# Loading the first x tile as two column halves from two queues, both ahead of the opening barrier

## The chip, the cores and the metric

One core of a Trainium2 chip. The metric is the device time of one execution in microseconds (us). The program runs on a single core.

## The reference

```python
def setup_inputs():
    batch, seq, dim = 32, 256, 1024
    return {"x": randn(batch, seq, dim) as float32, "y": the same shape}

def reference(x, y):
    result = zeros((batch, seq, dim * 2), float32)
    result[..., 0::2] = x
    result[..., 1::2] = y
    return result
```

67 MB are read and 67 MB written. There is no arithmetic, only an interleave.

## The kernel before

The flat arrays are cut into eight blocks of 128 rows of 8192 numbers (32 KB a row, 4 MB a tile). SyncE issues the loads and ScalarE the stores; VectorE writes x and y into the even and odd places of an output tile, twice for each block. The x, y and output pools have two buffers each. At the program's start stands an opening barrier, at which the engines wait for one another; the first x load is issued ahead of it.

```python
    WL = 8192
    WS = 4096
    ...
    zero = wpool.tile([16, 128], fp32, name="zero")
    nc.vector.memset(zero, 0.0)
    first = dataclasses.replace(of, offset=0, ap=[[2 * WL, 16], [1, 128]])
    nc.scalar.dma_start(out=first, in_=zero)      # small early store, overwritten later

    start = 0
    for lw in lwidths:                            # 8 x 8192
        xtile = xpool.tile([P, WL], fp32, name="xtile")[:, :lw]
        ytile = ypool.tile([P, WL], fp32, name="ytile")[:, :lw]
        xs = dataclasses.replace(xf, offset=start, ap=[[lw, P], [1, lw]])
        ys = dataclasses.replace(yf, offset=start, ap=[[lw, P], [1, lw]])
        nc.sync.dma_start(out=xtile, in_=xs)
        nc.sync.dma_start(out=ytile, in_=ys)
        soff = 0
        while soff < lw:                          # two output tiles a block
            ...
            nc.vector.tensor_copy(out=otile[:, 0::2], in_=xsub)
            nc.vector.tensor_copy(out=otile[:, 1::2], in_=ysub)
            nc.scalar.dma_start(out=os_, in_=otile)
            soff += width
        start += P * lw
    ...
    # after scheduling: the first SyncE load is moved ahead of SyncE's
    # arrival at the opening barrier
    opening.insert(gate, moved)
```

Of the kernel before, what the change touches and what calls it, by code (L numbers as in the profile page):

```python
# [3 lines left out]

# [4 lines left out]


@with_exitstack
def _interleave(
    ctx: ExitStack,
    tc: tile.TileContext,
    x: bass.AP,
    y: bass.AP,
    out: bass.AP,
):
    nc = tc.nc  # L20
    P = 128

    total = 1
    for s in x.shape:
        total *= s

    WL = 8192
    WS = 4096

    xf = x.rearrange("b s d -> (b s d)")  # L30
    yf = y.rearrange("b s d -> (b s d)")
    of = out.rearrange("b s d -> (b s d)")

    fp32 = mybir.dt.float32

    xpool = ctx.enter_context(tc.tile_pool(name="xp", bufs=2))
    ypool = ctx.enter_context(tc.tile_pool(name="yp", bufs=2))
    opool = ctx.enter_context(tc.tile_pool(name="op", bufs=2))

    lwidths = [WL] * (total // P // WL)  # L40
    assert sum(lwidths) == total // P


    wpool = ctx.enter_context(tc.tile_pool(name="wp", bufs=1))
    zero = wpool.tile([16, 128], fp32, name="zero")
    nc.vector.memset(zero, 0.0)  # L46
    first = dataclasses.replace(of, offset=0, ap=[[2 * WL, 16], [1, 128]])
    nc.scalar.dma_start(out=first, in_=zero)

    start = 0  # L50
    for lw in lwidths:
        xtile = xpool.tile([P, WL], fp32, name="xtile")[:, :lw]
        ytile = ypool.tile([P, WL], fp32, name="ytile")[:, :lw]

        xs = dataclasses.replace(xf, offset=start, ap=[[lw, P], [1, lw]])
        ys = dataclasses.replace(yf, offset=start, ap=[[lw, P], [1, lw]])
        nc.sync.dma_start(out=xtile, in_=xs)
        nc.sync.dma_start(out=ytile, in_=ys)

        soff = 0  # L60
        while soff < lw:
            width = min(WS, lw - soff)
            otile = opool.tile([P, 2 * WS], fp32, name="otile")[:, : 2 * width]
            os_ = dataclasses.replace(
                of,
                offset=2 * start + 2 * soff,
                ap=[[2 * lw, P], [1, 2 * width]],
            )
            xsub = xtile[:, soff : soff + width]
            ysub = ytile[:, soff : soff + width]  # L70
# [6 lines that stand above are left out]
    assert start == total  # L77


def kernel(tc, x, y, out):  # L80
    nc = tc.nc
    _interleave(tc, x, y, out)
    tc.close()
    tc.compile()  # L84


    blocks = nc.main_func.blocks
    opening = blocks[0].instructions
    at, moved = next(
        (b, i)  # L90
        for b in blocks[1:]
        for i in b.instructions
        if i.engine == mybir.EngineType.SP and i.opcode == "DMACopy"
    )
    assert not moved.sync_info.on_wait
    body = at.instructions
    body.remove(moved)
    gate = next(
        n
        for n, i in enumerate(opening)  # L100
        if i.engine == mybir.EngineType.SP and i.opcode == "Drain"
    )
    opening.insert(gate, moved)
    at.instructions = body
    blocks[0].instructions = opening




    last = nc.main_func.blocks[-1]  # L110
    tail = last.instructions
    wait = tail[0]
    clear = next(n for n, i in enumerate(tail) if i.opcode == "ISA")
    assert wait.engine == mybir.EngineType.SP and wait.opcode == "Drain"
    assert wait.sync_info.on_wait and not wait.sync_info.on_update
    assert tail[clear].engine == mybir.EngineType.Pool
    last.instructions = [
        copy.replace(wait, engine=mybir.EngineType.Pool)
    ] + tail[clear:]


# [1 line left out]
_INS = ['x', 'y']  # L123
_OUTS = [((32, 256, 2048), 'float32')]


# [23 lines left out]
```

## Time and profile before

| | before |
|---|---|
| time, median of the first 3 runs | 316.17 us (315.44 to 316.24) |
| span in the profile | 313.6 us |
| 16 DMA engines, both queues | 99.6% of the span |
| mean rate, and from 30 to 310 us | 428 and 434 GB/s |
| VectorE | 23% |

The first line is the whole execution, the second the profiled one from the first to the last instruction. The third line is the one that counts: the packets that the DMA engines move fill next to all of the span, so a change gains only if it takes idle time or work from them. The lines behind this table are in the prediction.

### The profile page before, as it was taken

What the parts mean: (1) busy time and instruction counts of PE and PEld (TensorE: products, weight loads), DVE (VectorE), ACT (ScalarE), POOL (GpSimd) and SP (SyncE); (2) the same over time, 40 slices, a digit from 0 to 9 for tenths busy, and PEclk for the clock granted to TensorE, in tenths of its full rate; (3) what the DMA queues carried; (4) which work ended last, traced back from release to release, by engine and by line L of the source; (5) the groups of instructions that cost most, each with busy time, mean ns of one, the idle gap of its engine ahead of it and who ended that gap; (6) DMA issues with size and microseconds to landing.
All of it is one profiled execution on the core that took longest, in us unless ns stands there. A gap on an engine that the chain in (4) does not pass through costs nothing.

```text
span 313.6 us, 140 instructions
## 1 busy us (share of the span) xinstructions
DVE 72.8 (23%) x33; POOL 0.2 (0%) x4
## 2 busy tenths in 40 slices
DVE  0433002231022410325003150131501305023500
POOL 0000000000000000000000000000000000000000
DMA  8999999999999999999999999999999999999997
GB/s 344 460 405 397 464 405 464 405 464 405 460 410 447 422 439 431 435 435 426 443 410 460 401 468 401 468 401 464 405 464 405 464 405 460 410 447 422 439 431 334
DMA packets 4640, 134.23 MB, mean 428 GB/s; under 512 B 528, under 2 KB 544, under 8 KB 544
## 3 DMA queue, kind: packets, MB, share of 16 engines
q1 hardware_dynamic: 2304, 67.11, 50.0%
q10 hardware_dynamic: 2336, 67.12, 49.6%
HBM read 67.11 MB, written 67.12 MB: 428 GB/s over the span
## 4 chain that ended last, share of the span: by engine, by line
DMA 83%; DVE 11%; DVEq 1%; issue 0%
DMA out_dram<-otile 76%; DMA ytile<-in_y_dram 7%; DVE otile L72 6%; DVE otile L71 5%; DVEq L84 1%; DVEq L71 0%
## 5 line engine op out<-in xcount | busy, mean ns | idle before, releaser
L71 DVE COPY otile<-xtile 128x4096 f32<-128x4096 f32 x16 | 36.6, 2295 | 184.8 <-DMA out_dram<-otile 173.6
L72 DVE COPY otile<-ytile 128x4096 f32<-128x4096 f32 x16 | 36.6, 2292 | 39.8 <-DMA ytile<-in_y_dram 39.8
L46 DVE MEMSET zero<- 16x128 f32 x1 | 0.2, 165 | 0.9 <-PEq L134 0.9
L134 POOL MEMSET const-bfloat16-1.0<- 128x1 bf16 x1 | 0.1, 101 | 0.0
L134 POOL MEMSET const-uint8-127<- 128x1 uint8 x1 | 0.1, 101 | 0.0
L134 POOL MEMSET const-float32-0.0<- 128x1 f32 x1 | 0.1, 98 | 0.2 <-issue 0.2
L134 POOL MEMSET const-float32-1.0<- 128x1 f32 x1 | 0.1, 98 | 0.0
## 6 DMA issues: line engine op xcount, KB each, us to landing
out_dram<-otile ACTq DMA_DIRECT2D x16, 4096.0 KB, 29.1
xtile<-in_x_dram SPq DMA_DIRECT2D x8, 4096.0 KB, 43.6
ytile<-in_y_dram SPq DMA_DIRECT2D x8, 4096.0 KB, 60.7
out_dram<-zero ACTq DMA_DIRECT2D x1, 8.0 KB, 6.3
```

Source lines behind the costliest of these rows:

```text
L46: nc.vector.memset(zero, 0.0)
L71: nc.vector.tensor_copy(out=otile[:, 0::2], in_=xsub)
L72: nc.vector.tensor_copy(out=otile[:, 1::2], in_=ysub)
L84: tc.compile()
L134: nc = _bacc.Bacc("TRN2", target_bir_lowering=False, num_devices=1)
```

## The change

The intent is a quicker start. The first x tile is the first thing that the kernel needs, and one queue brings it. With two queues, each with a half and each issued before the barrier, the data might flow sooner. The small zero store moves behind ScalarE's half.

```diff
-    nc.scalar.dma_start(out=first, in_=zero)
 ...
-        nc.sync.dma_start(out=xtile, in_=xs)
+        if start == 0:
+            for q, c in ((nc.sync, 0), (nc.scalar, lw // 2)):
+                q.dma_start(
+                    out=xtile[:, c : c + lw // 2],
+                    in_=dataclasses.replace(xf, offset=c, ap=[[lw, P], [1, lw // 2]]),
+                )
+            nc.scalar.dma_start(out=first, in_=zero)
+        else:
+            nc.sync.dma_start(out=xtile, in_=xs)
         nc.sync.dma_start(out=ytile, in_=ys)
 ...
-    (move the first load of SP ahead of the barrier)
+    for engine in (mybir.EngineType.SP, mybir.EngineType.Activation):
+        (move that engine's first load ahead of the barrier)
```

More of the change, by code (lines that the diff above doesn't have):

```diff
@@ L87 @@
     blocks = nc.main_func.blocks
-    opening = blocks[0].instructions
-    at, moved = next(
-        (b, i)
-        for b in blocks[1:]
-        for i in b.instructions
-        if i.engine == mybir.EngineType.SP and i.opcode == "DMACopy"
-    )
-    assert not moved.sync_info.on_wait
-    body = at.instructions
-    body.remove(moved)
-    gate = next(
-        n
-        for n, i in enumerate(opening)
-        if i.engine == mybir.EngineType.SP and i.opcode == "Drain"
-    )
-    opening.insert(gate, moved)
-    at.instructions = body
-    blocks[0].instructions = opening
+    for engine in (mybir.EngineType.SP, mybir.EngineType.Activation):
+        opening = blocks[0].instructions
+        at, moved = next(
+            (b, i)
+            for b in blocks[1:]
+            for i in b.instructions
+            if i.engine == engine and i.opcode == "DMACopy"
+        )
+        assert not moved.sync_info.on_wait
+        body = at.instructions
+        body.remove(moved)
+        gate = next(
+            n
+            for n, i in enumerate(opening)
+            if i.engine == engine and i.opcode == "Drain"
+        )
+        opening.insert(gate, moved)
+        at.instructions = body
+        blocks[0].instructions = opening
     last = nc.main_func.blocks[-1]
```

## The prediction

> **What bounds the kernel now.** The kernel moves 67 MB in, interleaves, and moves 67 MB out. I read the page first: busy time of the engines, the 40 slices, the queues.
>
> ```profile
> span 313.6 us, 140 instructions
> DVE 72.8 (23%) x33; POOL 0.2 (0%) x4
> DMA  8999999999999999999999999999999999999997
> q1 hardware_dynamic: 2304, 67.11, 50.0%
> q10 hardware_dynamic: 2336, 67.12, 49.6%
> HBM read 67.11 MB, written 67.12 MB: 428 GB/s over the span
> ```
>
> VectorE, the only computing engine, is busy for 23% of the span. The two DMA queues (q1 is SyncE's with the loads, q10 ScalarE's with the stores) together take 50.0 + 49.6 = 99.6% of the time of all 16 DMA engines. Only the first and the last slice are under nine tenths. So before any chain is looked at, the transfers are the bound, and the question is how much of the span they don't use. I next asked for stretches of the span (columns: stretch, VectorE, GpSimd, clock, DMA share, GB/s).
>
> ```profile
> 0.00:3.50 3.50, 0.17 (x1) 0.20 (x4) 1.00 0.88 300
> 3.50:24.00 20.50, 6.55 (x3) 0.00 (x0) 1.00 1.01 435
> 24.00:30.00 6.00, 2.44 (x2) 0.00 (x0) 1.00 0.92 350
> 30.00:310.00 280.00, 63.62 (x28) 0.00 (x0) 1.00 1.00 434
> 310.00:313.60 3.60, 0.00 (x0) 0.00 (x0) 1.00 0.49 209
> ```
>
> From 30 to 310 us the 16 engines are full at 434 GB/s with no gap. Below that rate are the start, a short stretch around 27 us, and the last microseconds. For these I read the trace's packet records one by one. A packet carries 32 KB, and past 30 us all 3,728 of them take 1.213 us. Each engine has 4096 / 16 = 256 of them, 256 x 1.213 = 310.5 us. The rest of the span: the first packet starts 0.99 us after the first issue; the first packets take about 1.9 us, 0.7 too long; around 27 us one packet per engine takes about 1.8 us, 0.6 too long (there the first large store joins the loads); from the last data packet's end at 312.70 to the end at 313.57 are 0.9 us. 310.5 + 1.0 + 0.7 + 0.6 + 0.9 = 313.7, against 313.6: the span is accounted for. Only 1.0 + 0.7 = 1.7 us of it are start-up.
>
> Then the start in order of time (start, length, engine, what).
>
> ```profile
> 0.00 0.37 SPq L57 DMA_DIRECT2D xtile<-in_x_dram  x1
> ...
> 0.78 0.33 SPq L58 DMA_DIRECT2D ytile<-in_y_dram  x1
> ...
> 1.06 0.42 ACTq L48 DMA_DIRECT2D out_dram<-zero  x1
> 1.16 0.42 SPq L57 DMA_DIRECT2D xtile<-in_x_dram  x1
> 1.63 0.51 SPq L58 DMA_DIRECT2D ytile<-in_y_dram  x1
> 12.23 4.50 DVE L71 COPY otile<-xtile 128x4096 f32<-128x4096 f32 x2 [11.20 <-DMA xtile<-in_x_dram]
> ...
> 21.95 4.50 DVE L72 COPY otile<-ytile 128x4096 f32<-128x4096 f32 x2 [5.22 <-DMA ytile<-in_y_dram]
> 24.27 33.70 ACTq L73 DMA_DIRECT2D out_dram<-otile  x3
> ```
>
> The first x load is already issued at 0.00, ahead of the barrier; y follows at 0.78. The x tile's copies run from 12.23 to 16.7 us, then VectorE waits 5.22 us for y, and only the y copies let the first store go. The chain of waits says the same: it goes through the first y load, not through x.
>
> ```profile
> 0.78 21.14 DMA ytile<-in_y_dram
> 21.92 0.02 issue
> 21.95 4.51 DVE otile L72 x2
> 26.45 0.02 issue
> 26.47 40.91 DMA out_dram<-otile
> ```
>
> **What the Trainium skill says.** "DMA: Bandwidth & Descriptors", section "Issuing engines are not separate DMA queues": transfers issued by the scalar and sync engines run on the same 16 DMA engines and interleave; issuing from several saves only the time of the sequencer's issue. The trace agrees: both queues' packets appear on the same engines, and an issue takes 0.33 to 0.51 us. The same page, section "Queues, rings and completion order": each DMA engine takes turns between queues by packets. The trace agrees in part: around 30 us packets of q1 and q10 alternate one by one, but a newly filled queue comes in late, the zero store issued at 1.06 shows its first packets at 5.27, and the first large store issued at 24.27 at 29.07. The same page, section "Where 436 GB/s comes from", has a ceiling of 435.2 GB/s; the 434 GB/s measured over 280 us is 99.7% of it, so the middle has nothing to give.
>
> **The change part by part.**
>
> Start of the data. The first x load (4 MB, 128 rows of 32 KB) becomes two of 2 MB, each with 128 rows of 16 KB. SyncE's half is issued at 0.00 as the whole was. Each half still has 128 rows, so I expect an issue of some 0.37 us for each, perhaps 0.42 where both are at it, as the overlapping zero store (ScalarE) and second x load (SyncE) show with 0.42 each. ScalarE stands at the barrier at 0.13 us in the raw instruction records, so its half goes out at 0.0 to 0.15. The first packet can't come sooner than SyncE's did, 0.99 us after its issue. The long first packet is a latency, and a second queue beside it helps only if its data come within the same latency. The packets of one queue already follow each other without a gap (first ends and second starts agree to some ns), so the engine had the next packet ready already. I credit 0.2 us out of the 1.7, with 0 to 0.5 possible.
>
> More packets. The records give 27 ns for a 512-byte packet and 1.213 us for 32 KB: 1186 ns for 32256 bytes more, so 27.2 bytes per ns and 8.2 ns fixed (an estimate from these two). Each engine gets 16 x-packets of 16 KB in place of 8 of 32 KB: 8 x 8.2 = 66 ns more, and one more completion packet of 9 ns: +0.08 us.
>
> Barrier. ScalarE arrives there some 0.4 us later than now. But SyncE itself arrives late now for the same reason: its issue ends at 0.37 and its drain at 0.55. So the release, now at about 0.7, moves by 0.05 to 0.2 us, and with it y's issue. The x halves keep the DMA engines busy for 4.19 MB / 434 GB/s = 9.7 us. Hidden entirely: 0.
>
> Landing of x. Both halves share the engines, so x as a whole lands near 12.2 us as now. If ScalarE's queue comes in late, as the records show for a new queue, its half lands up to 2 or 3 us later and y packets go first. Then the second x copy would end at about 17 to 18 us; the slack before y is 5.2 us. Cost 0, and no gain either if x is early. y needs the same 8.4 MB ahead of its end and lands at about 21.9 as now.
>
> Zero store. It moves behind ScalarE's x half, and lands perhaps at 13 to 16 us in place of 7.4. ScalarE's first large store waits for it, but goes only at 24.27: 8 us of slack, cost 0. The copies, the 16 stores and the other 15 loads keep their order and waits; the instruction order of the built kernel shows nothing else moved.
>
> Sum: -0.2 + 0.08 = -0.1 us.
>
> **The rivals.** (1) The intent comes true: two queues fill the engines sooner, all of the 0.7 us of first-packet excess goes, or the 0.6 at 27 us goes since ScalarE's queue has then carried large packets before. For it: the 27 us pause comes exactly where that queue first carries much. Against it: the zero store has used the queue already, and what is new at 27 us is a large read from SBUF and write to HBM, which the change leaves. Time if both went: 316.17 - 1.3 = 314.9. (2) A lost start: ScalarE reaches its issue late, or the two issues hold each other up (0.42 against 0.33), the barrier slips and the halves interleave badly. Every known term lies under the 9.7 us of queued x, so at most some 0.5 us: 316.7. (3) A new order of packets makes the DMA engines run dry later, or the first store late: the slack of 5.2 us ahead of y speaks against it, and SyncE's queue already holds the second x and y, 8.4 MB or 19 us of work. If y came 2 us later after all, the loads behind would still fill the engines; 316 to 317.
>
> **Range and chances.** The three runs of before are 315.44, 316.24 and 316.17, mean 315.95, so the median stands at the upper end of its own scatter of 0.8 us. From 315.95 the -0.1 leads to 315.9 (315.85 rounded). The range takes the scatter of about 0.5 on either side and 0.3 for the start: 315.1 to 316.7. Two per cent are 6.3 us, while all that isn't streaming at full rate is 3.1 us: faster by over 2% is not to be had by anything that leaves the bytes as they are. Slower by 2% would need the DMA engines idle for 6 us. One chance in a hundred for each.
>
> **What would show it.** In the profile after: issues of both halves in the first 0.6 us, y's issue at 0.8 to 1.0; x complete at 12 to 15 us; VectorE still waiting for y, with y complete at 21.5 to 22.2; the first store issued within 0.5 us of 24.3; 434 GB/s from 30 to 310 us; a span of 313.0 to 314.0. The pause at 27 us should still be there. Wrong would be: a DMA share under 0.95 anywhere between 4 and 24 us, an x half that lands after y, a span shorter by over 1 us (then the first packets or the 27 us pause were the cost of a fresh queue), or a drop in the steady rate.

## The result, and the profile after

The changed kernel takes 315.70 us in the median of 6 runs (315.48 to 315.91), the kernel before 316.21 in the same rounds (315.44 to 316.38). The ratio is 0.9989, with a 95% interval of 0.9977 to 1.0002. Ratios here are the mean time of one kernel's runs over that of the other's of the same rounds, so not quite the ratio of the medians. The interval holds 1, and a second set of rounds (below) gave 1.0001. The time is the same.

The page after, the same lines as were read before:

```profile
span 313.8 us, 141 instructions
DMA  8999999999999999999999999999999999999997
q10 hardware_dynamic: 2480, 69.22, 51.1%
q1 hardware_dynamic: 2304, 65.01, 48.4%
```

2.1 MB moved from q1 to q10, that is, ScalarE's half. The sum is 99.5% where it was 99.6%. The span is 0.2 us longer in this one profiled execution, not shorter. By stretches (stretch, VectorE, GpSimd, clock, DMA share, GB/s):

```profile
0.00:3.50 3.50, 0.17 (x1) 0.20 (x4) 1.00 0.74 239
3.50:24.00 20.50, 6.44 (x3) 0.00 (x0) 1.00 1.03 442
24.00:30.00 6.00, 2.56 (x2) 0.00 (x0) 1.00 0.96 360
30.00:310.00 280.00, 63.60 (x28) 0.00 (x0) 1.00 1.00 433
310.00:313.80 3.80, 0.00 (x0) 0.00 (x0) 1.00 0.58 250
```

The long middle is unchanged, 433 against 434 GB/s. The first stretch looks worse (0.74 against 0.88) and the second better (1.03 against 1.01). Both come from how the view counts: a packet (one record of the trace, a row of 32 KB or here also of 16 KB that one DMA engine moves) is put down to the moment it starts, and with 16 KB packets fewer bytes have "started" by 3.5 us. Counted by the time that the packets really ran, the share up to 3.5 us is 0.64 before and 0.65 after. For such short stretches the packet records are the better witness, and they show a first packet at 1.02 us (0.99 before) and 0.64 us too much for each engine in the first packets (0.65 before). Such an excess is the time of all packets over the usual 1.213 or 0.611 us, summed and divided by 16, as the records carry no engine's number. The start in order of time:

```profile
0.00 0.37 SPq L59 DMA_DIRECT2D xtile<-in_x_dram  x1
0.12 0.38 ACTq L59 DMA_DIRECT2D xtile<-in_x_dram  x1
...
0.92 0.33 SPq L66 DMA_DIRECT2D ytile<-in_y_dram  x1
...
11.72 4.50 DVE L79 COPY otile<-xtile 128x4096 f32<-128x4096 f32 x2 [10.55 <-DMA xtile<-in_x_dram]
...
22.06 4.49 DVE L80 COPY otile<-ytile 128x4096 f32<-128x4096 f32 x2 [5.85 <-DMA ytile<-in_y_dram]
24.39 33.74 ACTq L81 DMA_DIRECT2D out_dram<-otile  x3
```

The second queue did go out early, at 0.12 us. VectorE could start on x 0.5 us earlier (11.72 against 12.23), and then waited 5.85 us for y in place of 5.22. But that was the first half alone. The two halves landed so (page, section 6: KB, us from issue to landing):

```profile
xtile<-in_x_dram SPq DMA_DIRECT2D x1, 2048.0 KB, 11.7
xtile<-in_x_dram ACTq DMA_DIRECT2D x1, 2048.0 KB, 13.4
```

ScalarE's half was thus there at 0.12 + 13.4 = 13.5 us, and x as a whole 1.3 us later than before (12.2). y is complete at 22.06 in place of 21.95, and the first store leaves 0.12 us later. The chain of waits still goes through the first y load, whose issue the barrier now holds 0.14 us longer:

```profile
0.92 21.12 DMA ytile<-in_y_dram
22.04 0.02 issue
```

So the first half of x came 0.5 us sooner and the second 1.3 us later, and neither mattered: no output tile can be stored before y is there, and y came at 22.0 us, when 8.4 MB had gone through the 16 engines.

### The profile page after: what moved, and what is told of

Its sections match the earlier page's. It is cut to its first block, busy times and chain, and to the rows that moved or that the text cites. A ratio compares the mean times of both kernels' runs of the same rounds, so it can differ in the third digit from the quotient of the medians.

```text
span 313.8 us, 141 instructions
## 1 busy us (share of the span) xinstructions
DVE 72.8 (23%) x33; POOL 0.2 (0%) x4
## 4 chain that ended last, share of the span: by engine, by line
DMA 83%; DVE 11%; DVEq 1%; issue 0%
DMA out_dram<-otile 76%; DMA ytile<-in_y_dram 7%; DVE otile L80 6%; DVE otile L79 5%; DVEq L92 1%; DVEq L79 0%
## 6 DMA issues: line engine op xcount, KB each, us to landing
xtile<-in_x_dram SPq DMA_DIRECT2D x1, 2048.0 KB, 11.7
xtile<-in_x_dram ACTq DMA_DIRECT2D x1, 2048.0 KB, 13.4
out_dram<-zero ACTq DMA_DIRECT2D x1, 8.0 KB, 14.8
```

## The experiments

The theory: the end is set by the bytes and packets that the 16 DMA engines have to move, plus 3 us in which they don't. Which queue brings the bytes, and when x, y or the first store come, is of no account as long as the engines never run dry. The main rivals: the second queue does gain something at the start; the chain through the first y load is the bound; splitting costs something.

**The split without the second queue.** Both halves from SyncE, both ahead of the barrier.

```diff
-            for q, c in ((nc.sync, 0), (nc.scalar, lw // 2)):
+            for q, c in ((nc.sync, 0), (nc.sync, lw // 2)):
...
-    for engine in (mybir.EngineType.SP, mybir.EngineType.Activation):
+    for engine in (mybir.EngineType.SP, mybir.EngineType.SP):
```

> The split alone: both halves of the first x tile from SyncE's queue, both ahead of the barrier; ScalarE issues nothing early. Theory (the DMA engines are full from the first packet on, and which queue carries the bytes is of no account): same time as before and as the change within 0.3 us; ratio to before 0.998 to 1.001; the halves complete one after the other, near 7.3 and 12.2 us, and y near 22.0. Rival (the second queue is what gained the 0.1%): as slow as before, 316.2, and the change's 315.7 not reached. Rival (the split costs): 316.5 or more.

Measured: 315.51 us (5 runs), ratio 0.9993 (0.9981 to 1.0005). The halves were in use at 7.53 and 12.26 us, y at 21.97. From one queue both halves thus land sooner than from two (11.7 and 13.5 us). The theory's numbers hold, and the rival that credits the second queue falls: with one queue the time is no longer.

**No early issue at all.** The kernel before without its move ahead of the barrier; the block that moves the load is deleted.

```diff
-    opening = blocks[0].instructions
-    at, moved = next(...)
-    ...
-    blocks[0].instructions = opening
```

> The kernel before with the early issue taken out: the first x load goes out after the barrier like everything else. Control for what a start of the data is worth. Theory: the start of the data moves by 0.6 to 0.8 us and nothing absorbs it, so the time grows by 0.6 to 0.8 us (ratio 1.002 to 1.0025). Rival (a start is absorbed by the slack in front of y or in the buffers): same time within 0.2 us.

Measured: 316.23 us, before 315.72 on the same chip; ratio 1.0013 (1.0001 to 1.0025), that is 0.0 to 0.8 us longer, 0.4 in the middle. x is issued at 0.73 us, the first packet starts at 1.72 in place of 0.99, and the last data packet ends at 313.55 in place of 312.70. In the traces the shift passes through whole: from the first packet to the end of the last are 311.8 us here and 311.7 before, so nothing made the late start good. In the times somewhat less of it shows, with an interval that holds the expected 0.6 to 0.8 but also the rival's 0.2 and less. So the rival of a start that is absorbed loses by the two traces; by the times alone it isn't excluded. The change didn't move the start of the data: SyncE's load was at 0.00 already.

**y ten microseconds later.** The changed kernel with the second x load ahead of the first y load.

```diff
             nc.scalar.dma_start(out=first, in_=zero)
+            ahead = xpool.tile([P, WL], fp32, name="xtile")[:, :lw]
+            nc.sync.dma_start(out=ahead, in_=(second x block))
         nc.sync.dma_start(out=ytile, in_=ys)
```

> The changed kernel with the second x load issued ahead of the first y load, so that y completes 9.7 us later (near 31.7 us) and the first store leaves near 34 instead of 24.4. Theory (only the filling of the DMA engines counts): the loads in the queue still cover the time until the stores come, the time stays within 0.5 us of the change, ratio to before 0.997 to 1.003. Rival (the chain of waits through the first y load is the bound, as the page prints it): 9.7 us longer, near 325.5, ratio 1.03.

Measured: 315.49 us (6 runs), ratio 0.9992 (0.9980 to 1.0004). Its start in order of time:

```profile
11.97 4.50 DVE L87 COPY otile<-xtile 128x4096 f32<-128x4096 f32 x2 [10.80 <-DMA xtile<-in_x_dram]
...
32.02 4.50 DVE L88 COPY otile<-ytile 128x4096 f32<-128x4096 f32 x2 [15.56 <-DMA ytile<-in_y_dram]
34.35 0.36 ACTq L89 DMA_DIRECT2D out_dram<-otile  x1
```

y comes 10.0 us later, the first store leaves 10.0 us later, and the time doesn't change. So the chain as the page prints it isn't the bound. It says what each instruction waited for, but the DMA engines were at other loads all that time. This is the plainest of the runs: if 10 us at this spot cost nothing, neither the 0.1 us that y lost nor the 0.5 us that the first half of x won can matter.

**Without the zero store.**

```diff
-            nc.scalar.dma_start(out=first, in_=zero)
```

> The changed kernel without the small zero store. Theory: the x half has already used ScalarE's queue and the zero store now lies off every path, so same time within 0.3 us, and the pause near 27 us (0.6 to 0.8 us of long packets for each engine) stays. Rival (the zero store is a first write that warms the way to memory): the pause near 27 us grows and the time with it, by 0.5 us or more.

Measured: 315.46 us, ratio 0.9991 (0.9979 to 1.0003); long packets near 27 us of 0.82 us for each engine, 0.78 in the change. The zero store warms nothing that can be seen here, and its move behind the x half costs nothing.

**The change once more.**

> The changed kernel once more, beside the runs of before on this chip, to narrow the ratio. Theory (nothing moved that the end depends on): ratio 0.998 to 1.001, median 315.4 to 316.0. Rival (a real gain of 0.5 us from the early second queue): ratio at or under 0.9985.

Measured: 315.88 us (315.65 to 316.01), before 315.56 in the same rounds; ratio 1.0001 (0.9986 to 1.0016). The rival of a real gain of 0.5 us falls, if only just: the interval reaches from 0.4 us faster to 0.5 slower. A gain as small as the 0.2 us that the prediction credits could not be seen in these times. The 316.21 of before in the first rounds was one of its own: the medians of before in four sets are 316.21, 315.72, 315.56 and 315.71.

**All loads in halves.** A large dose of the one cost that the prediction gave the change.

```diff
-        else:
-            nc.sync.dma_start(out=xtile, in_=xs)
-        nc.sync.dma_start(out=ytile, in_=ys)
+        for tile_, flat in ((xtile, xf), (ytile, yf)):
+            (not the first x tile, which is in halves already)
+            for c in (0, lw // 2):
+                nc.sync.dma_start(out=tile_[:, c : c + lw // 2], in_=(that half))
```

> The changed kernel with all the other 15 loads cut in two column halves as well, both from SyncE's queue: a large dose of the one cost that the prediction gave the change. Theory (a packet costs 8.2 ns beside its bytes, a completion 9 ns): each DMA engine gets 15 x 8 = 120 more packets and 15 more completions, 0.98 + 0.14 = 1.1 us, so near 316.8 and ratio to before 1.0035 (1.002 to 1.005); the 16 KB packets take 0.611 us. Rival (packets of 16 KB are free, the fixed part overlaps): same time within 0.3 us. Rival (shorter packets are much worse): over 2 us.

Measured: 322.41 us (4 runs), ratio 1.0207 (1.0187 to 1.0226), 6.5 us more. The 16 KB packets do take 0.611 us, as expected, but that makes 1.1 us. The expectation was wrong: something else came in. Two things had changed beside the packets. With 15 more transfers SyncE's loads share completion semaphores with stores (a semaphore is a counter that a transfer raises when it has landed, and for which an instruction can wait). The load issued at 39.56 us, for one, waits for semaphore 105, which the store issued at 19.68 raises. SyncE's waits show it (what waits, for what: us in all, times, longest):

```profile
SPq L68 <- DMA out_dram<-otile: 122.0, 12, 16.9
```

And a load packet is now half as long as a store packet. The last two runs below were made to tell these apart.

**A wider zero store.** 8 KB in each of its rows in place of 512 bytes.

```diff
-    zero = wpool.tile([16, 128], fp32, name="zero")
+    zero = wpool.tile([16, 2048], fp32, name="zero")
-    first = dataclasses.replace(of, offset=0, ap=[[2 * WL, 16], [1, 128]])
+    first = dataclasses.replace(of, offset=0, ap=[[2 * WL, 16], [1, 2048]])
```

> The changed kernel with the zero store widened from 512 bytes to 8 KB in each of its 16 rows (0.13 MB more to write, 0.3 us at 434 GB/s). Asks what the pause at the first large store is. Theory a (a cost of the first store packets of some size, which an early store can pay while x loads run): the pause of 0.65 to 0.8 us for each engine shrinks below 0.3 us there. Theory b (it belongs to the first large store whatever went before): the pause stays at 0.6 to 0.85 us. Either way the time stays within 0.5 us of the change, since the early store then pays it instead.

Measured: 315.93 us, ratio 1.0007 (0.9991 to 1.0022); the pause near 27 us is 0.72 us for each engine. It can't be paid ahead in this way. Theory b fits here, though not all that follows: see below.

**The intent taken further.** The whole x from SyncE and the whole y from ScalarE, both ahead of the barrier.

```diff
+        nc.sync.dma_start(out=xtile, in_=xs)
+        if start == 0:
+            nc.scalar.dma_start(out=ytile, in_=ys)
+            nc.scalar.dma_start(out=first, in_=zero)
+        else:
+            nc.sync.dma_start(out=ytile, in_=ys)
```

> The intent taken further: the whole first x load from SyncE and the whole first y load from ScalarE, both ahead of the barrier, 8.4 MB in two queues in place of 4.2. Theory (only the filling of the DMA engines counts): x and y share the engines and complete together near 20 to 22 us, the first store leaves some 3 us later than in the change, and the time stays within 0.3 us (ratio 0.998 to 1.001); the first packet starts at 1.0 us as before. Rival (an early second queue gains at the start): over 0.5 us faster than before. Rival (the later first store delays the end): 3 us slower.

Measured: 315.93 us, ratio 1.0005 (0.9990 to 1.0020). The first packet starts at 1.00 us, x is complete at 21.84, the first store leaves at 26.37, 2.0 us later than in the change. Twice as much in the second queue gains nothing, and the later store costs nothing that the interval shows (0.3 us faster to 0.6 slower). What the expectation didn't foresee: the excess of long packets around the first large store is 1.4 us for each engine, twice that of the change, and the last data packet of the trace ends 0.4 us later.

**Small packets on both sides.** Back to the packets, on the kernel before: loads and stores in 16 KB packets, with no more transfers than before. Padding in the middle of each tile row breaks it in two; the addresses in DRAM stay.

```diff
-        xtile = xpool.tile([P, WL], fp32, name="xtile")[:, :lw]
+        xtile = xpool.tile([P, 2, WS + 16], fp32, name="xtile")[:, :, :WS]
-        xs = dataclasses.replace(xf, offset=start, ap=[[lw, P], [1, lw]])
+        xs = dataclasses.replace(xf, offset=start, ap=[[lw, P], [WS, 2], [1, WS]])
(the same for y, and for otile and its store)
```

> The kernel before with all loads and all large stores in 16 KB packets and the same number of transfers, same addresses in DRAM (the tiles have 64 bytes of padding in the middle of each row, so that a row of 32 KB goes as two pieces). The waits and the order of instructions stay. Theory (a packet costs 8 to 9 ns beside its bytes, nothing else changes where loads and stores have packets of one size): 256 more packets for each DMA engine, 256 x 9 ns = 2.3 us, so near 318.0 and ratio 1.0073 (1.006 to 1.009), no new pauses. Rival a (16 KB packets are bad in themselves, as the 6.5 us of the run with halved loads might be read): 10 us or more. Rival b (free): same time.

Measured: 317.11 us, ratio 1.0041 (1.0028 to 1.0054), about 1.3 us more. All 8192 data packets of loads and large stores are of 16 KB, 0.611 us in the median. The theory has the direction and about half the size. Its 9 ns a packet is right for a packet by itself, yet the end comes 1.4 us later in the trace (314.12 against 312.70), of which 0.4 us are the start: one issue of 256 pieces takes 0.62 us in place of 0.37, and the first packet starts at 1.40. Where packets of two queues take turns, they overlap a little more than before (1.9 us in all where it was 0.8), so that some 1.0 us is left for 256 packets, 4 ns each. Rivals a and b both fall.

**Small packets in the loads only.** The same padding in the x and y tiles alone; transfers, waits and order as before.

```diff
(the x and y lines of the diff above; otile and its store as before)
```

> The kernel before with only the loads in 16 KB packets, the stores in 32 KB, the same number of transfers and the same waits (padding in the x and y tiles only). It splits the 6.5 us of the run with all loads halved, of which only 1.1 us are packets. Theory a (the rest came from SyncE's waits for completion semaphores of stores, since that run had 15 more transfers): only the packets remain, 128 x 9 ns = 1.15 us, near 316.9, ratio 1.0036 (1.002 to 1.005). Theory b (the rest came from the turns: a load packet of 16 KB against a store packet of 32 KB gives the stores two thirds of the bytes, so the stores run ahead, their queue stands empty for long stretches and each return costs a pause): 3 us or more, ratio over 1.008, with stretches of 8 us and more without store packets in the trace.

Measured: 326.80 us (326.15 to 327.91), ratio 1.0360 (1.0341 to 1.0380), 11 us more. The program has the waits of before, and SyncE waits for no store in the trace. Theory a falls as the only cause. Theory b's turns and empty stretches are there. The two queues between 31 and 55 us, both busy (packets, MB, share), first with small packets on both sides, then in the loads only:

```profile
q10 hardware_dynamic: 336, 5.24, 51.0%
q1 hardware_dynamic: 332, 4.98, 48.5%
```

```profile
q10 hardware_dynamic: 225, 6.85, 66.1%
q1 hardware_dynamic: 229, 3.49, 33.9%
```

The two queues have nearly equal numbers of packets in both runs (some dozens are completions of 4 bytes), but in the second the stores get 6.85 of 10.34 MB, 66%, the two thirds of theory b. They run ahead, VectorE waits for the loads (114.8 us for y in all, where it was 39.8), the store queue stands empty for 9 to 10 us out of 39, and toward the end the loads are late. The stretches of this run at 286, 296 and 304 us:

```profile
286.00:296.00 10.00, 0.00 (x0) 0.00 (x0) 1.00 0.98 423
296.00:304.00 8.00, 3.36 (x2) 0.00 (x0) 1.00 0.33 139
304.00:324.30 20.30, 3.34 (x2) 0.00 (x0) 1.00 0.90 387
```

The last load packets end at 300.3 us, the last stores can't go before VectorE has copied them, and the DMA engines are at a third of their time. The kernel before has 438 GB/s in that stretch:

```profile
296.00:304.00 8.00, 2.28 (x2) 0.00 (x0) 1.00 1.02 438
```

The sum for each engine, from the packet records against before: packets 128 x 9 ns = 1.2 us, idle 6.4 (0.4 of it the later first packet, nearly all the rest between 296 and 304 us), long packets 3.6 (most of them where the store queue first comes or comes back), a little more overlap -0.5; 10.7 us, and the last data packet ends 10.75 us later. So the pauses at each return, which theory b named, are the smaller part; the larger is the idle time near the end, which it didn't name. For the run with all loads halved, the same sum against the change is packets 1.2, idle 2.4, long packets 3.8, overlap -0.4; 7.0 us, and the last data packet ends 7.0 us later. That the turns alone can do this is shown by this run. What part SyncE's 122 us of semaphore waits had in the other isn't: they were there as well, and that run was the faster of the two.

No run was faster than before or the change beyond its interval, so there is no better version to show.

## Why the prediction was right

The predicted time was 315.9 in 315.1 to 316.7; 315.70 was measured, and 315.88 the second time. The mechanism was right: the engines stayed full, and no term of the change reached the end. The sum of -0.1 us itself was not put to the test, since these times can't tell it from 0; its larger term did not come about, as said below.

*The bound.* It rested on the span's sum, 310.5 us of packets and 3.1 us of everything else. That the sum closes to 0.1 us is in part luck. It leaves out three terms that nearly cancel: 0.3 us of completion packets, 0.6 of idle time at the two ends, where not all engines are at work, and -1.0 of packets that overlap. It also takes as seen that both queues use the same engines; the records carry no engine's number, and it is read from 16 packets or a few more being in flight all the time from 4 to 296 us. The run with y 10 us later confirms that the chain of waits has to be read below this sum. The two runs with unequal packets show the other side. With small packets in the loads only, the engines ran dry for 6 us and the time went up by 3.6%. The prediction's condition that 2% slower would need 6 us of idle engines is too narrow, though: with all loads halved it was 2.1% with 2.4 us of idle time, since long packets took 3.8 us. The prediction had no such term.

*Start of the data, -0.2 us credited.* This small step failed. The issues took 0.37 and 0.38 us, as expected, and ScalarE's was at 0.12. But the first packet starts no sooner (1.02 us), the excess in the first packets is 0.64 in place of 0.65, and ScalarE's first packet starts only at 2.78. No gain is to be seen; from run to run this excess lies between 0.5 and 0.8. So here the excess was the same whether the first packet had 16 or 32 KB, and a second queue beside it shortened nothing.

*Packets, +0.08 us.* The 16 KB packets took 0.611 us, so 16 x 0.611 - 8 x 1.213 = 0.07 us for each engine. With small packets on both sides, the net cost is some 4 ns a packet, so the true figure may be half of that; too small to be seen in the time either way.

*Barrier, 0.* It opened 0.14 us later (y's issue at 0.92 in place of 0.78), within the 0.05 to 0.2 given. y was complete 0.11 us later; the run with y 10 us later shows that this costs nothing.

*x, zero store, first store.* The prediction allowed for ScalarE's half to be late, and it was: it landed 13.4 us after its issue, so at 13.5, 1.8 us after SyncE's; the zero store 14.8 us after 1.20, at 16.0, the upper end of what was said. Both had their slack, and the run without the zero store shows the last to be free.

*The pause at 27 us.* The prediction expected it to stay, against its own rival that a queue used before would not show it. It stayed, 0.78 us for each engine in place of 0.65. All the long packets there are load packets (in the kernel before 22 of them, started from 25.9 to 27.7 us), after the store's issue and ahead of its first packet at 29.07. The size differs more than the prediction had it: 0.6 us with small packets on both sides, 1.2 in the two runs with small packets in the loads alone, 1.4 with the whole y in ScalarE's queue. The wording that it comes from the first large store is too narrow: in the run with small load packets, four of the returns of the store queue after 9 to 10 us without store packets came with pauses of 0.4 to 0.6 us, while the returns after 2 us in the kernel before show none. Two more returns after such a gap had less (0.22 us at 147, 0.04 at 68 us), so the rule behind it stays open.

*The scatter.* The guess that the median of before stood high was right; later sets of before had medians of 315.56 to 315.72. Why runs of before scatter by 0.9 to 1.3 us in every set, and those of the change by 0.4, no run says.

## What to carry to other kernels

Where the DMA engines are full from the first packet to the last, as here, ask of an earlier issue how far it brings the very first packet forward. The second queue of this case didn't bring it forward at all. Test the bound by moving a link of the printed chain by a large amount and seeing whether the end moves. Look at the sizes of the packets that compete in two queues before cutting one side smaller: the change's own 16 KB packets met mostly each other and were harmless, while 16 KB packets in all loads came with 6.5 to 11 us more.

## What the Trainium skill lacked or had wrong

- "DMA: Bandwidth & Descriptors", section "Queues, rings and completion order", says that an engine takes turns between queues by packets, and gives a packet typically 9 to 17 descriptors. Here the turns are by single rows: from 38 to 44 us of the kernel before, 16 records of 32 KB from one queue, one for each engine, are followed by 16 from the other. It doesn't say what follows: with 16 KB packets in one queue and 32 KB in the other, the bytes went 34 to 66, and the kernel took 3.6% longer, while 16 KB in both cost 0.4%. Nor does it say how late a newly filled queue joins. Here 1.8 us passed between the first packets of the two queues when they were issued 0.12 us apart, and 3.4 to 4.8 us between issue and first packet where the other queue was running, with 16 KB packets as with 32 KB.
- The same page, section "Why small descriptors are slow (HBM only)", gives a fixed cost of about 3 cycles a packet, but no time for it. The records give 27 ns for 512 bytes, 611 ns for 16 KB and 1213 ns for 32 KB, so 8 to 9 ns fixed, of which some 4 ns a packet came through in the time with 256 more packets for each engine.
- The same page, section "Issuing engines are not separate DMA queues", calls the time of issue small. What no page has is how it grows: 0.37 us for the first load of 128 pieces, 0.62 for one of 256 (0.33 and 0.54 for later ones), and the first packet at 1.40 in place of 0.99 us.
- No page has the pause of 0.6 to 1.4 us for each engine at the first large store, and of 0.4 to 0.6 us at some later returns of stores after 9 to 10 us without them.
